# Attention values by whole rows, wider row projections, and half of each expert gather amid the gate/up products

## The chip, the cores and the metric

The kernel runs on one core of a Trainium2 chip. The metric is the device time of one execution in microseconds (us). The core has five engines that work side by side: TensorE (PE) for matrix products, VectorE (DVE), ScalarE (ACT), GpSimd (POOL) and SyncE (SP), whose queue issues nearly all transfers. Matrix products are written to PSUM and copied from there to SBUF by ACT or DVE.

## The reference

One layer of a hybrid decoder block over 512 tokens of width 1024, in float32:

```python
h = rmsnorm(x, g_mix);  proj = h @ w_in       # q, k, v, gates of both branches
o_g = gated_linear_attention(...)             # 4 heads, chunks of 64
o_m = moba_attention(...)                     # 8 heads of 64, blocks of 256, causal + top-3 past blocks
x = x + (sigmoid(z_g) * (o_g @ w_proj_gla) + sigmoid(z_m) * (o_m @ w_proj_moba)) @ w_out
x = x + memory_attention(rmsnorm(x, g_cross)) # 4 heads of 128 into 256 memory tokens
xt = rmsnorm(x, g_moe)                        # top-1 of 4 groups, top-2 of its 8 experts
for e in range(32):                           # for the tokens that chose expert e
    y[tok] += ((silu(xt[tok] @ w_gate[e]) * (xt[tok] @ w_up[e])) @ w_down[e]) * weight
out = rmsnorm(x + y, g_final)
```

The weights of the 32 experts (1024 x 512, 1024 x 512 and 512 x 1024 each) are 201 MB of the 252 MB that are moved.

## The kernel before

**Products.** Ordinary projections are made in three parts (`mm3`, lines 131 to 133): operands are split into a high part in the type fp32r and a rest, and high x high, rest x high and high x rest are added in PSUM. `in_feat` has weights as the stationary operand and 512 tokens moving (tiles `fo`). `in_rows` has 128 tokens as the stationary operand and the weights moving (tiles `ro0` to `ro3`); it goes over 256 columns at a time, in two loads of four k blocks (a k block is 128 of the 1024 features), and is called twice for the 512 columns of each of `vg`, `vm` and `vc`. `mm` (line 136) is a product in full float32; where its output has only 64 partitions (tiles `mo_ps`, `gu_ps`, `y_ps`), two such products lie side by side in the array's columns, which the rows show as `128*64`.

**Stages** on TensorE: rows and first projections to 39 us; projections woven with gated linear attention to 174; block attention (`moba`) woven with the gates' projections to 301; the two output projections, `w_out`, and memory attention with routing to 500; experts to the end.

**Block attention.** The items are 4 head pairs x 4 query tiles of 128. For each, `scores` (tile `s_ps`), a softmax on ACT and DVE, transposes of the probabilities (`ptp`), copies by ACT (`pt`), and `values` (`mo_ps`) for that query tile. The values of an item stand behind the scores of the next one. Between them the weaving puts products of the gates (`fo`).

**Experts.** The 32 experts are taken as 16 pairs p. Each expert has 64 slots, so a pair fills 128 partitions. `gate_up` makes gate and up products for one k block (`gu_ps`; 8 k blocks make 64 records). `hidden` (ACT, DVE) and `hidden_t` (four transposes `ht_ps` and a copy) follow, then `down` (`y_ps`, 32 records), a split into high and rest (`yh`, `yl`), and `combine`: for four token tiles and two column halves a product with the slots' rows (`c_ps`), added to x by DVE. The inputs of four experts are gathered at once by products with one-hot rows (`gather`: 8 chunks, one a k block, `g_ps`, copied to `xT`). For the experts of pairs p + 2 and p + 3, four chunks are made after the gate/up products of even pair p and four after those of pair p + 1, in alternation with the steps of `combine`, so that both cover `hidden`.

**Order of transfers.** A pair has 24 weight blocks of 512 KB, 384 in all, and each takes one of 48 buffers of the pool `blk`, which also holds other tiles. `eload(n)` lets SP issue all up to number n; it is called after k blocks and after `down` steps with `used + DEPTH + ...`, and for pair 0 with the list `D0`. The overflow loop (`overflow`, line 1268) handles experts with over 64 tokens; its count is read from memory into registers, and on the inputs here it runs zero times. It stands at the start of pair 15. The loads from number 368 on are held back until it is passed.

**Tail.** The last pair's `down` goes by two column halves. Each half has its own products and additions; squares are summed by ACT, the power of -1/2 is made on POOL (`rr`), and two stores of 256 KB go out for each token tile.

The routing codes are spread over all partitions by `c_bcast` (transposes `cb_ps` and copies), between the gate/up products of pair 0.

## Time and profile before

| what | value |
| --- | --- |
| median of 3 runs | 985.75 us (985.1 to 986.44) |
| the profiled execution | 985.1 us, with a span of 983.3 us on the core |
| TensorE busy | 961.1 us, 98% of the span, 5305 matmuls |
| VectorE, ScalarE, GpSimd busy | 474.8, 311.7, 32.7 us |
| moved by DMA | 252.52 MB, 257 GB/s over the span |

The span runs from the first to the last instruction. Busy time counts an engine as busy while at least one of its instructions is under way. Matmuls overlap, so the duration of a single one is longer than its distance to the next. PEld stands for the weight loads of TensorE, which lie beside its products.

### The profile page before, as it was taken

To read this page: it belongs to the slowest core of one execution; us is meant where nothing else is said; L and a number is where in the kernel's file an instruction comes from. 1 tells how busy PE (TensorE), PEld (TensorE's weight loads), DVE (VectorE), ACT (ScalarE), POOL (GpSimd) and SP (SyncE) were. 2 spreads that over 40 slices of the span, in tenths; PEclk is the share of its full clock that TensorE was granted. 3 is DMA by queue.
4 is the path that set the end of the run, shared out by engine and by line. 5 is a ranking of instruction groups with operands and counts; after the bars stand their busy time and mean duration, and the time that the engine had idled before them with its cause. 6 is when DMAs were issued, how large, how long until landed. Compare 5 with 4: busy or idle time off the path is not lost. (4 is left out here: it accounts for less than half of the span.)

```text
span 983.3 us, 13899 instructions
## 1 busy us (share of the span) xinstructions
PE 961.1 (98%) x5305; PEld 645.5 (66%) x5305; DVE 474.8 (48%) x1048; ACT 311.7 (32%) x631; POOL 32.7 (3%) x46
## 2 busy tenths in 40 slices
PE   9999999999999999999999999999999999999985
PEld 7889779888788888999844555544555554455432
DVE  6343863345555746566752543434453333444314
ACT  5452633445446424455521111111111111111003
POOL 3200010000000000000000000000000000000003
PEclk9999999999999999999999999999999999999998
DMA  9512347133133522644588999999999999999993
GB/s 300 160 44 58 71 65 193 44 86 86 60 133 129 176 81 67 198 190 196 200 331 329 409 408 409 409 409 408 409 409 409 409 408 409 409 409 409 409 383 148
DMA packets 117161, 252.52 MB, mean 257 GB/s; under 512 B 10310, under 2 KB 61795, under 8 KB 117092
## 3 DMA queue, kind: packets, MB, share of 16 engines
q1 hardware_dynamic: 117092, 251.60, 69.3%
q8 instruction: 43, 0.70, 0.3%
q14 instruction: 26, 0.21, 0.1%
HBM read 247.90 MB, written 3.67 MB: 256 GB/s over the span
## 5 line engine op out<-in xcount | busy, mean ns | idle before, releaser
L136 PE MATMUL gu_ps<-we,xT 128*64 128x512 f32 x1024 | 229.3, 597 | 5.1 <-PEq L1268 3.8
L136 PEld LDWEIGHTS gu_ps<-we,xT 128*64 128x64 f32 x1024 | 78.0, 138 | 150.5 <-issue 134.6
L213 DVE TENSOR_TENSOR wlo<-wraw,whi 128x1024 fp32r<-128x1024 f32 (+1 forms) x71 | 86.6, 1238 | 90.0 <-ACT whi L212 89.8
L136 PE MATMUL y_ps<-we,hid_t 128*64 128x512 f32 x512 | 114.2, 595 | 0.3 <-issue 0.3
L1229 DVE SCALAR_TENSOR_TENSOR hid<-hid,ws,gu_ps 128x512 f32<-128x512 f32 x16 | 11.9, 747 | 194.9 <-PE gu_ps L136 194.9
L1262 DVE TENSOR_TENSOR x<-c_ps,x 128x512 f32<-128x512 f32 x120 | 76.7, 685 | 38.9 <-PE c_ps L136 38.9
L131 PE MATMUL fo<-hTh,whi 128*128 128x512 f32 x224 | 90.5, 404 | 0.0
L133 PE MATMUL fo<-hTh,wlo 128*128 128x512 f32 x224 | 87.5, 391 | 0.0
L132 PE MATMUL fo<-hTl,whi 128*128 128x512 f32 x224 | 87.4, 390 | 0.0
L136 PEld LDWEIGHTS y_ps<-we,hid_t 128*64 128x64 f32 x512 | 36.3, 137 | 68.8 <-issue 55.7
L212 ACT ACTIVATE whi<-wraw 128x1024 fp32r<-128x1024 f32 (+2 forms) x73 | 74.5, 1043 | 1.9 <-DMA wraw<-in_w_in_dram 1.8
L1228 ACT ACTIVATE hid<-gu_ps 128x512 f32<-128x512 f32 x16 | 9.6, 597 | 197.5 <-PE gu_ps L136 197.5
L136 PE MATMUL g_ps<-oh,xrh 128*128 128x256 f32 x256 | 64.6, 293 | 1.7 <-DVE oh L1030 1.7
L136 PE MATMUL g_ps<-oh,xrl 128*128 128x256 f32 x256 | 61.6, 281 | 0.0
L136 PEld LDWEIGHTS g_ps<-oh,xrh 128*128 128x128 f32 x256 | 47.0, 189 | 14.9 <-PE gu_ps L136 9.7
L133 PE MATMUL ro<-whi,hTl 128*128 128x256 f32 (+1 forms) x192 | 55.4, 289 | 0.8 <-DVE hTl L333 0.8
L131 PE MATMUL ro<-whi,hTh 128*128 128x256 f32 (+1 forms) x192 | 56.0, 291 | 0.0
L132 PE MATMUL ro<-wlo,hTh 128*128 128x256 f32 (+1 forms) x192 | 55.5, 289 | 0.2 <-POOL wlo L213 0.2
L212 ACT ACTIVATE yh<-y_ps 128x512 fp32r<-128x512 f32 x32 | 19.1, 598 | 109.9 <-PE y_ps L136 109.9
L136 PE MATMUL c_ps<-yh,ot 128*128 128x512 f32 x128 | 50.8, 397 | 0.7 <-ACT yh L212 0.7
L136 PE MATMUL c_ps<-yl,ot 128*128 128x512 f32 x128 | 50.8, 397 | 0.2 <-DVE yl L213 0.2
L131 PEld LDWEIGHTS fo<-hTh,whi 128*128 128x128 f32 x224 | 42.0, 188 | 12.0 <-issue 3.9
(320 smaller groups left out, 1544.5 us busy)
## 6 DMA issues: line engine op xcount, KB each, us to landing
we<-in_w_exp_gate_dram SPq DMA_DIRECT2D x128, 512.0 KB, 10.2
we<-in_w_exp_up_dram SPq DMA_DIRECT2D x128, 512.0 KB, 10.2
we<-in_w_exp_down_dram SPq DMA_DIRECT2D x128, 512.0 KB, 10.2
wraw<-in_w_in_dram SPq DMA_DIRECT2D x38, 512.0 KB, 3.8
wraw<-in_w_out_dram SPq DMA_DIRECT2D x8, 512.0 KB, 6.1
wraw<-in_w_ckv_dram SPq DMA_DIRECT2D x8, 512.0 KB, 4.6
wraw<-in_w_proj_gla_dram SPq DMA_DIRECT2D x4, 512.0 KB, 3.9
wraw<-in_w_proj_moba_dram SPq DMA_DIRECT2D x4, 512.0 KB, 4.3
```

The source lines that it names most:

```text
L131: PE.matmul(o, lh, rh, start=first, stop=False)
L132: PE.matmul(o, lh, rl, start=False, stop=False)
L133: PE.matmul(o, ll, rh, start=False, stop=last)
L136: PE.matmul(o, l, r, start=first, stop=last, **kw)
L212: S.activation(hi, src, AF.Copy)
L213: eng.tensor_tensor(lo, src, f(hi), op=ALU.subtract)
L1228: S.activation(row, gu[0][0:n], AF.Silu)
L1229: V.scalar_tensor_tensor(row, row, ws[:, 0:1], gu[1][0:n], op0=ALU.mult, op1=ALU.mult)
L1262: V.tensor_tensor(xs, o, xs, op=ALU.add)
```

## The change

- `in_rows` goes over 512 columns at once, in four loads of two k blocks (`WIDE`).
- The mean square of the second token tile is made by ACT inside `to_feat`, not by DVE ahead of it.
- In block attention, the transposed probabilities of all query tiles of a head pair are kept (`pa`, `pb`), and `values` runs once per head pair, over all queries from key block j on.
- The broadcast of the codes begins between the two halves of the routing's last gather, and the tables of slots follow two k blocks earlier in pair 0.
- A gather belongs to an odd pair p and the pair after it: four chunks after the gate/up products of p, as before, and four ahead of the k blocks 0 to 3 in the gate/up products of p + 1. Pair 0 has no gather, and pair 14 has one's second half.
- `DEPTH` is 35 for pair 0 and 33 behind it. The overflow loop moves into pair 15, ahead of k = 2; its count is read at the start of pair 14, it has its own PSUM tiles, and loads from number 372 on are held back until it is passed.
- In the last pair the down weights are loaded by column halves; output goes by the column ranges 512, 256 and 256; the sums of squares have three parts; and one store of 512 KB goes out per token tile (two of 256 KB for the last).

The core of the diff (the removed lines of the old block attention and of the old tail are left out):

```diff
+    add_rows(w_in, 512, 512, WIDE)
...
-    def in_rows(n, evac, src, nt=NT, mark=None):
-        acc = [ps(f"ro{t}", [n]) for t in range(nt)]
-        for kh in range(2):
-            wh, wl = wnext(4, n)
+    def in_rows(evac, src, nt=NT, mark=None):
+        acc = [ps(f"ro{t}", [512]) for t in range(nt)]
+        kk = 0
+        for kn in WIDE:
+            wh, wl = wnext(kn, 512)
             for t in range(nt):
-                for k in range(4):
-                    kk = 4 * kh + k
-                    mm3(acc[t], src.hi[kk][:, tcol(t)], src.lo[kk][:, tcol(t)], wh[:, k, :], wl[:, k, :], kk == 0,
-                        kk == KD - 1)
-                    yield 0.33
-                if kh:
+                for k in range(kk, kk + kn):
+                    mm3(acc[t], src.hi[k][:, tcol(t)], src.lo[k][:, tcol(t)], wh[:, k - kk, :], wl[:, k - kk, :], k == 0,
+                        k == KD - 1)
+                    yield 0.65
+                if kk + kn == KD:
                     evac(t, acc[t])
+            kk += kn
...
+    def between():
+        r1.append(rms_scale(x_in[1]))
+        wsplit(2)
+    to_feat(xr, hT, 0, between)
+    rows[1] = scaled_rows(x_in[1], r1[0], gmix)
...
+        def transposed(i, res, pts):
+            for (pr, _), (pa, pb) in zip(res, pts):
                 t_ps = ps("ptp", [i + 1, P])
                 for j in range(i + 1):
                     PE.transpose(t_ps[:, j, :], pr[:, tcol(j)], ident)
+                n = min(i + 1, 2)
+                S.activation(pa[:, 0:n, tcol(i)], t_ps[:, 0:n, :], AF.Copy)
+                if i > 1:
+                    S.activation(pb[:, 0:i - 1, tcol(i - 2)], t_ps[:, 2:i + 1, :], AF.Copy)
+        def values(hp, pts):
+            o_ps = ps("mo_ps", [T])
+            for j in range(NT):
                 for half in range(2):
                     h = 2 * hp + half
                     sl = slice(64 * half, 64 * half + 64)
+                    pa, pb = pts[half]
+                    p_j = pa[:, j, j * P:] if j < 2 else pb[:, j - 2, (j - 2) * P:]
+                    mm(o_ps[sl, j * P:], vm[j][:, h * 64:(h + 1) * 64], p_j, j == 0, j == NT - 1, skip_group_check=True)
+            split(om.hi[hp], om.lo[hp], o_ps)
         items = [(hp, i) for hp in range(4) for i in range(NT)]
+        prev = None
         for hp, i in items:
             res = scores(hp, i)
+            if prev and i == 0:
+                values(*prev)
             yield 0.64 * FILL[i][0]
             normalise(i, res)
             yield 0.64 * FILL[i][1]
+            if i == 0:
+                prev = hp, [(blk("pa", [2, T]), med("pb", [2, 2 * P])) for half in range(2)]
+            transposed(i, res, prev[1])
         yield 1.0
+        values(*prev)
...
+    def load_down_halves(e):
+        for c in range(2):
+            for q in range(2):
+                b = blk("we", [2, 512])
+                rows = w_exp_down[0][e][2 * q * P:(2 * q + 2) * P, 512 * c:512 * c + 512]
+                SY.dma_start(b, rows.rearrange("(k p) n -> p k n", p=P))
+                yield b
...
-    eloads, elimit = [0], [12 * (NE - 2) + SPILL_AT]
+    eloads, elimit = [0], [SPILL[2]]
     def load_pairs():
         for p in range(NE // 2):
             pair = 2 * p, 2 * p + 1
-            for loads, n in ((load_gate_up, 2), (load_down, 1)):
+            for loads, n in ((load_gate_up, 2), (load_down_halves if p == NE // 2 - 1 else load_down, 1)):
...
+    bcast = c_bcast()
+    steps(bcast, 2)
     c_weights()
     c_gather(NT - 1)
...
+            if len(xT) == k:
+                xT.extend(rows2("xT", 4, ns))
+            o = to[k % 2] if to else ps("g_ps", [ns])
...
     NP = NE // 2
-    bcast, slot, spill = c_bcast(), None, spill_list()
+    slot, spill = None, spill_list()
     comb, gat = iter(()), iter(())
-    xT_next = None
     for p in range(NP):
         w = blocks[2 * p:2 * p + 2]
         used = 24 * p
-        if p == NP - 1:
-            eload(elimit[0])
-            overflow(*spilled)
-            elimit[0] = 12 * NE
-        eload(used + D0[0] if p == 0 else used + DEPTH)
-        if p % 2 == 0 and p:
-            xT = xT_next
+        depth = DEPTH[min(p, 1)]
+        if p == SPILL[0] - 1:
+            n_extra = nc.values_load(spilled[0][0:1, 0:1], min_val=0, max_val=NX - 1, skip_runtime_bounds_check_because=
+                                     "2 T assignments fill fewer than NX whole blocks")
+        eload(used + depth)
         gu = [ps("gu_ps", [512]) for q in range(2)]
         s0 = (p % 2) * P
         for k in range(KD):
+            if (p, k) == SPILL[0:2]:
+                overflow(n_extra, *spilled)
+                elimit[0] = 12 * NE
+            if p % 2 == 0:
+                steps(gat, 1)
             gate_up(gu, k, [xT[k][:, s0 + CAP * i:s0 + CAP * i + CAP] for i in range(2)], w)
             if k % 2:
-                eload(D0[1 + k // 2] if p == 0 else used + DEPTH + 2 * (k + 1))
+                eload(used + depth + 2 * (k + 1))
             if p == 0 and k >= BC_AT:
                 next(bcast, None)
-                if k == BC_AT + 3:
+                if k == BC_AT + 1:
                     slot = slot_rows(sid[:, 0:1])
-                    oh_next = group_hots(1)
-        if p % 2 == 0 and p + 2 < NP:
-            xT_next = rows2("xT", KD, 4 * CAP)
-            gat = gather(oh_next, xT_next, 4 * CAP)
+            if p % 2 and p + 1 < NP and k == OH_AT:
+                oh_next = group_hots((p + 1) // 2)
+        if p % 2 and p + 1 < NP:
+            xT = []
+            gat = gather(oh_next, xT, 4 * CAP)
         if p == NP - 1:
             gf = blk("gf", [D])
             SY.dma_start(gf, bcast_rows(g_final, D))
         hid = hidden(gu, slot[1])
-        gs = 4 if p + 2 < NP else 0
-        steps(gat, min(gs, 1))
+        gs = 1 if p % 2 and p + 1 < NP else 0
+        steps(gat, gs)
         steps(comb, 2 if gs else 4)
         hid_t = hidden_t(hid)
         for i in range(3):
-            steps(gat, min(gs, 1))
+            steps(gat, gs)
             steps(comb, 2)
         drain(comb)
         ot = slot[0]
         if p + 1 < NP:
             slot = slot_rows(sid[:, 2 * p + 2:2 * p + 3])
-        if p % 2 and p + 3 < NP:
-            oh_next = group_hots((p + 3) // 2)
         if p >= 2:
...
+    ranges = (0, 512), (512, 256), (768, 256)
...
     def scale(t):
+        V.tensor_tensor(s01[t], s01[t], ssq[t][:, 2:3], op=ALU.add)
+        G.tensor_tensor(r[t], s01[t], neghalf[:, 0:1], op=ALU.pow)
+    def low_half(t):
+        S.activation(xo[t][:, 0:512], xo[t][:, 0:512], AF.Copy, scale=r[t])
+    def high_half(t):
+        V.scalar_tensor_tensor(xo[t][:, 512:], x_sb[t][:, 512:], r[t], gf[:, 512:], op0=ALU.mult, op1=ALU.mult)
+    last_down(0, range(4))
+    high(0)
+    low(0)
+    last_down(1, range(4))
+    high(1)
+    low(1)
+    last_down(2, range(2))
+    o0 = products(0)
+    o1 = products(1)
+    last_down(2, range(2, 4))
+    for t in range(NT):
+        add(o0, 0, t)
+        if t == NT - 1:
+            high(2)
+        square(0, t)
+        gains(t)
+    for t in range(NT):
+        add(o1, 1, t)
+        square(1, t)
+        if t == 0:
+            low(2)
+    o2 = products(2)
+    for t in range(NT):
+        V.scalar_tensor_tensor(s01[t], ssq[t][:, 0:1], EPS, ssq[t][:, 1:2], op0=ALU.add, op1=ALU.add)
+        add(o2, 2, t)
+        square(2, t)
+        if t == 2:
+            scale(0)
+            low_half(0)
+    for t in range(NT):
+        high_half(t)
+        if t + 1 < NT:
+            SY.dma_start(out[tcol(t), :], xo[t])
+            scale(t + 1)
+            low_half(t + 1)
+    S.dma_start(out[tcol(t), 0:512], xo[t][:, 0:512])
+    SY.dma_start(out[tcol(t), 512:], xo[t][:, 512:])
...
+WIDE = 2, 2, 2, 2
+SPILL = 15, 2, 372
...
-DEPTH = 30
-D0 = 34, 37, 41, 44, 47
+DEPTH = 35, 33
+OH_AT = 3
```

TensorE's order in block attention, at the end of the first head pair; `ptp` are the transposes, `s_ps` the scores of the next item, `mo_ps` the values and `fo` the gates' products. Before, for query tile 3 (the last ahead of the next head pair):

```order
L133 MATMUL fo<-hTh_145,wlo 128x512
L679 MATMUL ptp<-keep,pr 128x128 x8
L136 MATMUL s_ps<-km_1092,qm_1412 128x256 x2
L136 MATMUL s_ps<-km_1093,qm_1412 128x256 x2
L136 MATMUL mo_ps<-pt,vm_1518 64x128 x4
L136 MATMUL mo_ps<-pt,vm_1519 64x128 x4
L131 MATMUL fo<-hTh_145,whi 128x512
L132 MATMUL fo<-hTl_149,whi 128x512
```

The change, for the same place, and behind it the place one query tile earlier:

```order
L133 MATMUL fo<-hTh_145,wlo 128x512
L675 MATMUL ptp<-keep,pr 128x128 x8
L136 MATMUL s_ps<-km_989,qm_1309 128x256 x2
L136 MATMUL s_ps<-km_990,qm_1309 128x256 x2
L136 MATMUL mo_ps<-pa,vm_1415 64x512 x2
L136 MATMUL mo_ps<-pa,vm_1415 64x384 x2
L136 MATMUL mo_ps<-pb,vm_1416 64x256 x2
L136 MATMUL mo_ps<-pb,vm_1416 64x128 x2
L131 MATMUL fo<-hTh_145,whi 128x512
```

```order
L133 MATMUL fo<-hTh_148,wlo 128x512
L675 MATMUL ptp<-keep,pr 128x128 x6
L136 MATMUL s_ps<-km_936,qm_1201 128x512 x2
L136 MATMUL s_ps<-km_937,qm_1201 128x512 x2
L131 MATMUL fo<-hTh_145,whi 128x512
L132 MATMUL fo<-hTl_149,whi 128x512
L133 MATMUL fo<-hTh_145,wlo 128x512
```

All values of the head pair now stand behind the first scores of the next one, eight products in a row over 512, 384, 256 and 128 columns in place of eight over 128, and behind the other query tiles' scores no values are left.

TensorE's order at the start of pair 2 (`y_ps` is the end of pair 1, `g_ps` a chunk of the gather). Before:

```order
L136 MATMUL y_ps<-we,hid_t 64x512 x16
L136 MATMUL gu_ps<-we,xT_5124 64x512 x16
L136 MATMUL gu_ps<-we,xT_5125 64x512 x16
L136 MATMUL g_ps<-oh,xrh_4067 128x256
L136 MATMUL g_ps<-oh,xrl_4071 128x256
L136 MATMUL g_ps<-oh,xrh_4068 128x256
L136 MATMUL g_ps<-oh,xrl_4072 128x256
L136 MATMUL g_ps<-oh,xrh_4069 128x256
```

The change:

```order
L136 MATMUL c_ps<-yh,ot 128x512
L136 MATMUL c_ps<-yl,ot 128x512
L136 MATMUL y_ps<-we,hid_t 64x512 x16
L136 MATMUL g_ps<-oh,xrh_3812 128x256
L136 MATMUL g_ps<-oh,xrl_3816 128x256
L136 MATMUL g_ps<-oh,xrh_3813 128x256
L136 MATMUL g_ps<-oh,xrl_3817 128x256
L136 MATMUL g_ps<-oh,xrh_3814 128x256
L136 MATMUL g_ps<-oh,xrl_3818 128x256
L136 MATMUL g_ps<-oh,xrh_3815 128x256
L136 MATMUL g_ps<-oh,xrl_3819 128x256
L136 MATMUL gu_ps<-we,xT_4950 64x512 x4
```

Eight gather products now stand ahead of each of the first four k blocks (`x4` are the four products of one k block), and none of them behind this pair's gate/up products.

SP's queue around the overflow loop, with the loads ahead of it. Before:

```order
L940 DMA we<-in_w_exp_up_dram 128x1024
L940 DMA we<-in_w_exp_gate_dram 128x1024
L940 DMA we<-in_w_exp_up_dram 128x1024
L1266 TENSOR_LOAD rt_xi
L1268 COMPARE_AND_BRANCH
L1268 UNCONDITIONAL_BRANCH
L1450 BRANCH_PREFETCH_HINT
L1269 ISA
L1269 TENSOR_LOAD rt_xi
```

The change:

```order
L935 DMA we<-in_w_exp_up_dram 128x1024
L935 DMA we<-in_w_exp_gate_dram 128x1024
L935 DMA we<-in_w_exp_up_dram 128x1024
L935 DMA we<-in_w_exp_gate_dram 128x1024
L1312 TENSOR_LOAD rt_xi
L935 DMA we<-in_w_exp_up_dram 128x1024
L935 DMA we<-in_w_exp_gate_dram 128x1024
L935 DMA we<-in_w_exp_up_dram 128x1024
L1273 COMPARE_AND_BRANCH
L1273 UNCONDITIONAL_BRANCH
L1496 BRANCH_PREFETCH_HINT
```

The read of the loop's count has moved ahead of the last three loads before the loop, and the loop's branch now stands behind four loads of pair 15.

## Rows read from the trace of the kernel before

**Rows 1.** The line of the page with the DMA rate in 40 equal slices of the span (24.6 us each), in GB/s.

```profile
GB/s 300 160 44 58 71 65 193 44 86 86 60 133 129 176 81 67 198 190 196 200 331 329 409 408 409 409 409 408 409 409 409 409 408 409 409 409 409 409 383 148
```

**Rows 2.** Busy time by stage: stretch in us, its length, then for PE, PEld, DVE, ACT and POOL the busy us with the number of instructions, the granted clock, the DMA share and GB/s. The stretches are block attention, the experts up to the last pair's y products, and the tail.

```profile
174.00:301.00 127.00, 125.99 (x711) 101.94 (x711) 62.30 (x211) 62.36 (x166) 0.00 (x0) 1.00 0.29 89
...
500.00:959.60 459.60, 453.90 (x2276) 216.96 (x2276) 181.99 (x373) 68.53 (x127) 0.00 (x0) 1.00 1.01 401
959.60:983.30 23.70, 12.32 (x49) 5.53 (x48) 10.85 (x21) 8.91 (x22) 7.59 (x8) 0.88 0.36 138
```

**Rows 3.** The same view for TensorE alone in two undisturbed stretches: the `vm` row projection (256 columns) and the `w_out` product (512 columns). Columns: length, busy us (records touched), granted clock, DMA share, GB/s.

```profile
153.94:176.97 23.03, 23.03 (x193) 1.00 0.49 128
345.08:366.85 21.77, 21.77 (x98) 1.00 0.28 77
```

**Rows 4.** Groups of instructions by line and shape in those two stretches: names, shape, count, busy us and mean ns of one, idle before.

```profile
L133 PE MATMUL ro<-whi,hTl 128*128 128x256 f32 x64 | 18.1, 283 | 0.0
...
L133 PE MATMUL xo<-whi,mTl 128*128 128x512 f32 x32 | 12.5, 389 | 0.0
```

**Rows 5.** Timeline of TensorE and ACT in block attention (start us, duration, engine, line, operation, and in brackets the idle time before with what ended it).

```profile
246.60 0.60 PE L136 MATMUL mo_ps<-pt,vm 128*64 128x128 f32 x4 [0.42 <-ACT pt L681]
...
270.65 1.09 ACT L681 ACTIVATE pt<-ptp 128x512 f32<-128x512 f32 x2 [0.94 <-PE ptp L679]
...
277.87 0.72 PE L136 MATMUL s_ps<-km,qm 128*128 128x256 f32 x4
278.52 0.46 PE L136 MATMUL mo_ps<-pt,vm 128*64 128x128 f32 x4
278.91 0.50 PE L131 MATMUL fo<-hTh,whi 128*128 128x512 f32 x1
279.25 0.39 PE L132 MATMUL fo<-hTl,whi 128*128 128x512 f32 x1
```

**Rows 6.** Timeline of DVE and TensorE at the start, where the first rows are projected.

```profile
10.80 0.74 DVE L333 TENSOR_TENSOR hTl<-tps,hTh 128x256 fp32r<-128x256 f32 x2
...
11.26 0.59 PE L133 MATMUL ro<-whi,hTl 128*128 128x272 f32 x1 [0.83 <-DVE hTl L333]
```

**Rows 7.** Timeline of TensorE around pair 0 of the experts.

```profile
499.89 5.37 PE L136 MATMUL gu_ps<-we,xT 128*64 128x512 f32 x24
505.20 0.65 PE L1073 MATMUL cb_ps<-keep,rt_code 128*128 128x128 f32 x4
505.78 1.94 PE L136 MATMUL gu_ps<-we,xT 128*64 128x512 f32 x8
507.64 0.65 PE L1073 MATMUL cb_ps<-keep,rt_code 128*128 128x128 f32 x4
...
516.71 0.39 PE L136 MATMUL g_ps<-oh,xrh 128*128 128x256 f32 x1
...
522.38 7.09 PE L136 MATMUL y_ps<-we,hid_t 128*64 128x512 f32 x32
529.29 13.90 PE L136 MATMUL gu_ps<-we,xT 128*64 128x512 f32 x64
```

**Rows 8.** Timeline of TensorE, DVE and ACT from the end of pair 1's gate/up products to pair 2's.

```profile
543.13 0.39 PE L136 MATMUL g_ps<-oh,xrh 128*128 128x256 f32 x1
...
543.30 0.75 DVE L1229 SCALAR_TENSOR_TENSOR hid<-hid,ws,gu_ps 128x512 f32<-128x512 f32 x1 [12.44 <-PE gu_ps L136]
...
545.11 0.60 PE L1235 MATMUL ht_ps<-keep,hid 128*128 128x128 f32 x4
545.47 0.36 PE L136 MATMUL g_ps<-oh,xrh 128*128 128x256 f32 x1
...
545.75 0.60 ACT L1237 ACTIVATE hid_t<-ht_ps 128x512 f32<-128x512 f32 x1 [0.89 <-PE ht_ps L1235]
...
551.28 7.09 PE L136 MATMUL y_ps<-we,hid_t 128*64 128x512 f32 x32
558.20 13.90 PE L136 MATMUL gu_ps<-we,xT 128*64 128x512 f32 x64
```

**Rows 9.** Busy time of TensorE in the gate/up products of pairs 12 to 15, and in two us of pair 15 (columns as in rows 3).

```profile
847.56:862.13 14.57, 14.57 (x66) 1.00 1.03 409
877.17:892.83 15.66, 15.11 (x66) 1.00 1.03 409
907.90:923.67 15.77, 15.12 (x66) 1.00 1.03 410
938.86:955.29 16.43, 16.43 (x64) 0.90 1.00 388
940.00:942.00 2.00, 2.00 (x6) 0.50 0.92 340
```

**Rows 10.** Timeline of TensorE, POOL and DVE in the last pair and the tail.

```profile
938.86 16.50 PE L136 MATMUL gu_ps<-we,xT 128*64 128x512 f32 x64 [3.77 <-PEq L1268]
...
959.63 5.98 PE L136 MATMUL y_ps<-we,hid_t 128*64 128x512 f32 x24
...
974.10 1.07 POOL L1382 TENSOR_TENSOR rr<-ms,neghalf 128x1 f32<-128x1 f32 x2 [1.95 <-DVE ms L1380]
...
974.69 0.75 DVE L1387 SCALAR_TENSOR_TENSOR xo<-x,rr,gf 128x512 f32<-128x512 f32 x1 [0.59 <-POOL rr L1382]
```

More of the change, by code (lines that the diff above doesn't have):

```diff
@@ L204, in block_kernel @@
     add_feat(w_cq, 0, 4)
-    for j in range(2):
-        add_rows(w_ckv, 512 + 256 * j, 256)
+    add_rows(w_ckv, 512, 512, WIDE)
     for c in range(2):
@@ L1085, in block_kernel @@
     c_exp(1)
-    steps(vgen, 16)
+    steps(vgen, 8)
     c_normalise(0)
@@ L1263, in combine, with overflow @@
                 yield t, c
-    def overflow(xi, xb):
-        n_extra = nc.values_load(xi[0:1, 0:1], min_val=0, max_val=NX - 1,
-                                 skip_runtime_bounds_check_because="2 T assignments fill fewer than NX whole blocks")
+    def overflow(n_extra, xi, xb):
         with tc.For_i(0, n_extra, 1, iteration_sync='staggered') as i:
@@ L1289, in overflow @@
                     gate_up(gu, k, xT[k:k + 1], [{2 * j + q: w[q] for q in range(2)}])
-            hid_t = hidden_t(hidden(gu, ws, CAP, hid), CAP)
-            y_ps, load = [ps("y_ps", [512]) for c in range(2)], load_down(bass.ds(e, 1), to)
+            hid_t = hidden_t(hidden(gu, ws, CAP, hid), CAP, pb[4][:, 0:4 * CAP].rearrange("p (a n) -> p a n", a=4))
+            y_ps, load = pb[0:2], load_down(bass.ds(e, 1), to)
             for ft in range(4):
@@ new lines, in block_kernel, with x_part, y_part, last_down @@
+    ssq, xo = [small("ss3", [3]) for t in range(NT)], [blk("xo", [D]) for t in range(NT)]
+    s01, r = [small("ss4", [1]) for t in range(NT)], [small("rr", [1]) for t in range(NT)]
+    def x_part(i, t):
+        a, n = ranges[i]
+        return x_sb[t][:, a:a + n]
+    def y_part(i):
+        a, n = ranges[i]
+        return y_ps[a // 512][:, a % 512:a % 512 + n]
+    def last_down(i, fts):
+        a, n = ranges[i]
+        c, a = divmod(a, 512)
+        for ft in fts:
+            for e, (b, own) in enumerate(zip(w, halves)):
+                mm(y_ps[c][own, a:a + n], hid_t[:, ft, 64 * e:64 * e + 64], b[8 + 2 * c + ft // 2][:, ft % 2, a:a + n],
+                   ft == 0, ft == 3, skip_group_check=True)
@@ new lines, in block_kernel, with high, low, products @@
+    y = [[med(q, [n], F32R) for q in ("yh", "yl")] for _, n in ranges]
+    def high(i):
+        S.activation(y[i][0], y_part(i), AF.Copy)
+    def low(i):
+        V.tensor_tensor(y[i][1], y_part(i), f(y[i][0]), op=ALU.subtract)
+    def products(i):
+        n = ranges[i][1]
+        o = [ps("c_ps", [512 // n, n]) for _ in range(NT * n // 512)]
+        o = [b[:, q, :] for b in o for q in range(512 // n)]
+        for t in range(NT):
+            product(o[t], ot, t, y[i])
+        return o
```

119 lines of the change are left out of this document (22 added, 97 removed).

## The prediction

> **What bounds the kernel now.** I first read the busy time of each engine by stage [rows 2]. TensorE is busy for 125.99 of 127.00 us in the block-attention stage and for 453.90 of 459.60 us in the expert stage, and it waits only at a few places. So a term counts if it changes how fast TensorE's stream runs, or one of its stops. Next comes the line of GB/s [rows 1]: from the 23rd slice on the weights arrive at 408 to 409 GB/s with hardly a gap. TensorE and the weights run neck and neck in the expert stage, and each gain there must be held against the other. Third, the late pairs [rows 9]: the 64 gate/up records of one pair take 13.84 us where nothing is late (529.29 in [rows 7] to 543.13 in [rows 8]), but 14.57, 15.66, 15.77 and 16.43 us in pairs 12 to 15. That is 7.1 us over the undisturbed time, and the weights are late there. Ahead of pair 15 stands a stop of 3.77 us at the overflow loop [rows 10], and in 940 to 942 us the granted clock is 0.50, that is 1.2 of 2.4 GHz [rows 9]. The profiled span is 983.3 us and this execution took 985.1, so 1.8 us lie outside. The median of the runs is 985.75, 0.65 above it. I add the sum to the median.
>
> **How to read TensorE's rows.** Durations overlap, so a price is the distance from one start to the next. 192 matmuls of 256 columns fill 23.03 us, 0.120 each, and 96 of 512 columns fill 21.77 us, 0.227 each [rows 3], though single ones are listed at 283 and 389 ns [rows 4].
>
> **1. Row projections 512 wide: -3.15 us.** 192 + 192 + 96 matmuls of 256 columns become 240 of 512: 480 x 0.120 = 57.6 against 240 x 0.227 = 54.4. Loads keep their number and size, and splits their work. Bounds 0 (if a split comes late) and -3.2. The listed durations would give 480 x 0.283 - 240 x 0.389 = 42.5 us. That reading is wrong, since the same rows would then need 54 us for a window of 23.03.
>
> The Trainium skill (TensorE: Matmul & The Clock Gate, section Single matmul latency) puts one matmul at (398 + N) / 2.4 ns. That is 272 and 379 ns, near the listed durations, and by it the term would be 39.6 us. The section Back-to-back issue gap of that page puts the distance at N / 2.4 + 2.5 ns, 109 and 216, by which it would be 0.6 us. The measured distances of 120 and 227 ns lie above both, and the sum goes by them.
>
> **2. Attention values once per head pair: -5.2 us.** The columns stay the same, but 12 of 16 visits to the 64-column form go away. One visit costs, beyond its columns [rows 5]: the four value records take 0.39 us (278.52 to 278.91) for 4 x 128 columns, which at 0.216 per 512 are 0.22, so 0.17 extra. The first fo after it takes 0.34 instead of 0.23, so 0.11. The scores ahead take 0.65 for 4 x 256 columns, 0.48, so 0.17, which may belong to the change of data type that stays. That makes 0.28 to 0.45 a visit. I take 0.37, and 12 x 0.37 = 4.4. A value record now and then waits for its copy (0.42 at 246.60). The copies of the first three query tiles lose their hurry, for which I estimate 1.2, three such places at 0.4 each. Against it the last tile needs four copies instead of two (1.09 us for two); behind 0.65 us of scores I let 0.1 a head pair show, 0.4. Bounds -2.5 and -6.6.
>
> **3. Mean square of the second tile on ACT: -0.5.** TensorE waits 0.83 us at 11.26 for hTl, which DVE begins at 10.80 behind that mean square [rows 6]. Bounds 0 and -0.9.
>
> **4. Broadcast of the codes: +1.45 ahead of the experts.** Eight transposes at 0.09 (four take 0.36, 545.11 to 545.47 [rows 8]) make 0.72, plus one copy that xT waits behind, an estimate with bounds 0.7 and 2.
>
> **5. Pair 0: -4.8.** It takes 29.40 now (499.89 to 529.29 [rows 7]). One interruption by four cb transposes costs 505.20 to 507.64, 2.44, less eight gate/up records of 0.216, which is 0.71 us. Two of the four leave, so gate/up takes 13.84 + 1.42 = 15.26. Without a gather nothing covers the hidden row. From [rows 8], DVE ends 0.92 after the last gate/up record (543.30 + 0.75 against 543.13), ht follows at 1.05, its copy ends 1.24 after that, and with 0.1 to spare y starts at 2.4. y takes 6.92 (551.28 to 558.20). Sum 24.6. The four chunks of this gather are not gone; the last gather's second half now lies in pair 14: 32 x 0.12 plus a switch, **+4.0**.
>
> **6. Half of each gather amid gate/up: +9.8.** In an even pair from 2 to 14 TensorE goes from 64-column products to full-width ones and back five times instead of once. A round trip is the interruption of term 5 without its own work: 0.71 - 0.36 = 0.35. 7 x 4 x 0.35 = 9.8. Bounds: 0.20 each (only the first g after gate/up, 0.10, and the way back), 5.6, and 0.45 as in term 2, 12.6. The copies of the chunks out of PSUM (some 0.6 us each, as that of hid_t in [rows 8]) have 1.7 us of gate/up beside them and are hidden; uncovered they would cost up to 28 x 0.6 = 17 us.
>
> The Trainium skill (TensorEngine Tiling (Array Packing), section Key Properties) says that a change of the tiling mode drains the array. It speaks against this edit and gives no price; the trace has one in the 0.35 above.
>
> **7. Deeper loads: -7.1.** The 7.1 us over in pairs 12 to 15 [rows 9] go if the weights come 4 to 6 us earlier against TensorE. They lost some 4.8 us in each of the slices at 331 and 329 GB/s (24.6 x 80 / 409), around pair 0, where loads waited for blocks that pair 0 and its gather held. Pair 0 is now shorter, holds fewer blocks and asks for one to three more. The slower even pairs add margin. Bounds -3 and -7.1.
>
> **8. Overflow loop in pair 15 behind two k: -1.9, then +0.9.** The registers are read a pair earlier. I halve the stop of 3.77 us [rows 10], with bounds of 1.3 and 3.8 for what is left, both estimates. SP is now stopped after load 371 instead of 367, until TensorE is two k into pair 15, so the queue runs dry for some 5 us; I charge 0.9 for a late weight at k = 6.
>
> **9. The tail: +0.3.** From the first y of the last pair (959.63 [rows 10]) to the end there are 23.7 us. Won: 0.7 of a wait for the last weight, and about 1 from a last range of 256 instead of 512 columns. Lost: the power on POOL (1.07 for two) now stands between one tile's last square and its 0.75 us on DVE, tile by tile, about 1.5 us a tile instead of 1.0. Bounds -1.5 and +2.
>
> **Sum.** -3.15 - 5.2 - 0.5 + 1.45 - 4.8 + 4.0 + 9.8 - 7.1 - 1.9 + 0.9 + 0.3 = -6.2, so 985.75 - 6.2 = **979.5 us**. The expert stage is nearly even (+1.2), and the gain is made ahead of it.
>
> **Rivals.**
> (a) *The switches are cheap.* At 0.20 each, term 6 is 5.6, and the time 975.3. For it: one part of the round trip is a gap of only 0.10. Against it: [rows 7] show the whole. Below that the weights bind: about 973.
> (b) *The loop costs what it did.* A stop of 3.9 again (+1.9) and half clock behind it again (16.43 x (1 - 0.90) = 1.6, which is part of the 7.1 in term 7): 983.0. For it: [rows 9, 10]. Against it: the registers are loaded early.
> (c) *The weights bind the end.* If term 7 brings only 3 and the dry queue costs 2 more: 979.5 + 4.1 + 2 = 985.6, no change.
> (d) *Slower: the values wait.* All four copies of a head pair's last tile stand on ACT ahead of all its values, behind the gates' work. If TensorE stands s us there each time, the gain is gone at s = 1.55, and at 2.5 the time is 989.5. For it: TensorE already waits 0.42 for one such copy [rows 5]. Against it: ACT is busy for only 62.36 of 127 us [rows 2].
>
> **Numbers.** The measurement tells 0.2% (2 us) from no change. The sum 0.50 (own range 977 to 982.5), (a) 0.20, (b) 0.15, (c) 0.07, (d) 0.08. Faster: 0.50 + 0.20 + two thirds of (b) = 0.80. Same: the rest of (b) and most of (c), 0.11. Slower: 0.09. The range 972 to 986 takes in all but (d) and the far end of (a).
>
> **What the profile after will show.** 1: v rows of 96 matmuls in 21.8 us. 2: the block-attention stage some 5 us shorter, with four value segments of about 2.4 us. 5: pair 0 in 24.6. 6: even pairs 1.4 us longer than odd ones. 7: gate/up of pairs 12 to 14 free of waits. 8: a stop under 3 us inside pair 15. I am wrong if even pairs are as long as odd ones, if the late pairs still wait, or if the gain ahead of the experts is under 6 us.

## The result, and the profile after

The changed kernel takes 979.11 us (median of 4 runs, 978.45 to 980.16), against 985.55 for the kernel before, measured beside it (4 runs, 985.1 to 986.44). The ratio is 0.9935, with a 95% interval of [0.9917, 0.9952]: 0.65% faster. The forecast was 979.5, faster. The profiled execution took 979.03 us with a span of 977.2, so the span is 6.1 us shorter. Each experiment below has its own measurements of the kernel before beside it, to which its ratio is taken; their medians lie between 984.79 and 985.36 us. A difference of under 1 us between two variants is therefore read from the traces and not from the times.

From the page of the changed kernel: the span, the busy time of the engines, and the DMA rate in 40 slices (24.4 us each).

```profile
span 977.2 us, 13312 instructions
PE 955.9 (98%) x4993; PEld 623.6 (64%) x4993; DVE 473.0 (48%) x1056; ACT 313.5 (32%) x648; POOL 32.2 (3%) x46
...
GB/s 295 168 44 65 65 61 185 57 83 91 61 182 127 193 21 132 135 276 133 256 315 409 409 409 409 409 409 409 409 409 409 409 409 409 409 409 409 409 307 129
...
L136 PE MATMUL gu_ps<-we,xT 128*64 128x512 f32 x1024 | 229.2, 595 | 0.7 <-ACT xT L1051 0.3
```

TensorE is still busy for 98% of the span. The full rate of 409 GB/s begins one slice earlier than in [rows 1], and the 39th slice falls to 307 (it was 383), because the last loads are held back until the loop. By the listed idle times the gate/up products stood for 0.7 us in the whole run. Before, pair 15's alone stood 3.77 [rows 10].

The stretches of the changed kernel on TensorE. Columns as in [rows 3]. In order: the `vm` projection, block attention from its first scores to the first output projection, memory attention's output up to the first gate/up product, pair 0, an odd pair, the even pair behind it, two stretches of pair 15, and the tail from the last pair's first y.

```profile
152.62:174.38 21.76, 21.76 (x98) 1.00 0.60 157
174.38:294.16 119.78, 118.80 (x593) 1.00 0.31 96
441.31:493.30 51.99, 49.73 (x344) 1.00 0.49 182
493.30:517.91 24.61, 22.99 (x109) 1.00 0.96 370
577.19:606.18 28.99, 28.99 (x150) 1.00 1.03 409
606.18:636.35 30.17, 30.17 (x150) 1.00 1.03 409
930.00:935.00 5.00, 5.00 (x26) 1.00 0.51 206
935.00:940.00 5.00, 5.00 (x26) 1.00 0.68 231
952.00:977.20 25.20, 11.94 (x73) 0.83 0.35 137
```

Three stretches of the kernel before that no row above has: block attention between the same two points, 25 us around the end of its pair 0, and the stretch up to its first gate/up product.

```profile
176.97:301.43 124.46, 123.45 (x691) 1.00 0.30 92
520.00:545.00 25.00, 25.00 (x129) 1.00 0.88 340
448.98:499.89 50.91, 48.85 (x336) 1.00 0.50 187
```

TensorE's longest stop in block attention of the changed kernel, ahead of the transposes of the probabilities:

```profile
201.95 0.63 PE L675 MATMUL ptp<-keep,pr 128*128 128x128 f32 x4 [0.33 <-DVE sm L666]
```

TensorE of the changed kernel in the last pair and the tail. Start us, duration, operation, idle before.

```profile
932.15 11.32 PE L136 MATMUL gu_ps<-we,xT 128*64 128x512 f32 x50
943.67 1.08 PE L136 MATMUL gu_ps<-we,xT 128*64 128x512 f32 x4 [0.20 <-DMA we<-in_w_exp_gate_dram]
944.95 2.79 PE L136 MATMUL gu_ps<-we,xT 128*64 128x512 f32 x10 [0.20 <-DMA we<-in_w_exp_up_dram]
...
952.00 5.38 PE L136 MATMUL y_ps<-we,hid_t 128*64 128x512 f32 x32
958.33 1.08 PE L136 MATMUL y_ps<-we,hid_t 128*64 128x256 f32 x8 [0.94 <-DVE yl L1388]
```

The 50 records from 932.15 to 943.47 run across the loop's place without a gap that the trace names, and the clock is 1.00 throughout. The stop of [rows 10] is gone. In its place there are two waits of 0.20 for weights, and a new stop of 0.94 in the tail. From start to start the two waits cost more than they are listed with. All gate/up products of pair 15, and two us around the loop's place:

```profile
932.15:947.67 15.52, 15.12 (x67) 1.00 0.76 269
934.00:936.00 2.00, 2.00 (x12) 1.00 0.10 35
```

They take 15.52 us where 13.84 would do, and the 1.7 us lie at k = 6, the first k block whose loads were held back: the queue had run almost empty (35 GB/s).

Where the span went, term by term, as distances between the same two instructions in both traces (us):

| term | forecast | measured | from |
| --- | --- | --- | --- |
| 1 wide rows | -3.15 | -3.05 | `vg` -1.17, `vm` 23.03 to 21.76, `vc` -0.61 |
| 2 values | -5.2 | -4.7 | 124.46 to 119.78 |
| 3 start | -0.5 | -0.2 | first rows done at 39.69 instead of 39.88 |
| 4 broadcast | +1.45 | +1.1 | 50.91 to 51.99 |
| 5 pair 0; chunks in pair 14 | -4.8; +4.0 | -4.8; +3.8 | 29.40 to 24.61; 32 x 0.12 |
| 6 amid gate/up | +9.8 | +9.7 | 7 x (59.16 - 57.78), two pairs after and before |
| 7, 8 late weights, loop | -8.1 | -9.2 | 4.5 of waits in pairs 12 to 14, 3.77, 16.43 to 15.52 |
| 9 tail | +0.3 | +1.5 | 23.67 to 25.20 |

The sum of the right column is -5.9, and the span lost 6.1. The rows are no closed account: ahead of pair 0 they add up to 6.85 where the first gate/up product comes 6.59 us earlier (499.89 to 493.30), and from there to the last pair's first y they add up to 0.5 where 1.0 was won (459.74 to 458.70). The 3.8 for the chunks in pair 14 is worked out and not measured.

### The profile page after: what moved, and what is told of

It is laid out like the page before. It is cut to its first block, busy times and chain, and to the rows that moved or that the text cites. A ratio compares the mean times of both kernels' runs of the same rounds, so it can differ in the third digit from the quotient of the medians.

```text
span 977.2 us, 13312 instructions
## 1 busy us (share of the span) xinstructions
PE 955.9 (98%) x4993; PEld 623.6 (64%) x4993; DVE 473.0 (48%) x1056; ACT 313.5 (32%) x648; POOL 32.2 (3%) x46
## 4 chain that ended last, share of the span: by engine, by line
PE 91%; DVE 3%; ACT 2%; DMA 2%; issue 1%; SPq 1%; POOL 0%; POOLq 0%; DVEq 0%; ACTq 0%
PE gu_ps L136 22%; PE y_ps L136 12%; PE fo L131 7%; PE fo L133 7%; PE fo L132 7%; PE g_ps L136 7%; PE c_ps L136 6%; PE ro L133 2%; PE ro L131 2%; PE ro L132 2%; PE x2o L136 2%; PE xo L132 1%; PE xo L133 1%; PE xo L131 1%; PE o_ps L136 1%; PE mo_ps L136 1%
## 5 line engine op out<-in xcount | busy, mean ns | idle before, releaser
L136 PEld LDWEIGHTS gu_ps<-we,xT 128*64 128x64 f32 x1024 | 70.9, 137 | 134.7 <-issue 121.5
L136 PE MATMUL y_ps<-we,hid_t 128*64 128x512 f32 (+1 forms) x528 | 113.9, 583 | 1.6 <-DVE yl L1388 0.9
L1209 ACT ACTIVATE xT<-g_ps,gfeat 128x256 f32<-128x256 f32 x56 | 25.8, 474 | 89.2 <-PE g_ps L136 57.6
L136 PE MATMUL c_ps<-yh,ot 128*128 128x512 f32 (+1 forms) x132 | 52.4, 399 | 0.5 <-ACT yh L1385 0.5
L136 PE MATMUL c_ps<-yl,ot 128*128 128x512 f32 (+1 forms) x132 | 51.0, 388 | 0.1
L133 PEld LDWEIGHTS fo<-hTh,wlo 128*128 128x128 f32 x224 | 42.1, 188 | 9.1
L136 PEld LDWEIGHTS g_ps<-oh,xrl 128*128 128x128 f32 x256 | 47.1, 189 | 0.6
```

What stands on the lines that cost most here:

```text
L133: PE.matmul(o, ll, rh, start=False, stop=last)
L136: PE.matmul(o, l, r, start=first, stop=last, **kw)
L1209: S.activation(xT[k], o, AF.Copy, scale=gfeat[:, k:k + 1])
```

## Experiments: what a visit amid gate/up costs

The theory: each return from the gather to the gate/up products costs 0.35 us, so the same eight chunks in fewer visits save that much per visit left out. The rival: the cost belongs to the chunks or their copies, and stays.

**Two visits of two chunks** instead of four of one.

```diff
-            if p % 2 == 0:
-                steps(gat, 1)
+            if p % 2 == 0 and k in (0, 2):
+                steps(gat, 2)
```

> Four chunks amid the gate/up products as in the changed kernel, but two ahead of k = 0 and two ahead of k = 2. By the price of a visit (0.345 us) even pairs are 0.69 shorter and the time is 4.8 us shorter, 974.3. If the price lies in the chunks (their copies, their weight loads) and not in the visit, nothing changes: 979.

Measured: 975.43 us, 0.9904 [0.9888, 0.9921]. An odd and an even pair of this run on TensorE:

```profile
576.87:605.89 29.02, 29.02 (x151) 1.00 1.03 409
605.89:635.38 29.49, 29.49 (x151) 1.00 1.03 410
```

The two take 58.51 us, 0.65 less for two visits fewer: 0.33 each. Over seven even pairs that is 4.6 us, of which 3.6 arrived in the span; 0.5 went to gate/up of pair 15, which took 16.03 instead of 15.52, with one wait of 0.51 for weights, and 0.35 was lost ahead of the experts (pair 0 begins at 493.65).

**Seven visits**: the four chunks amid gate/up in seven pieces.

```diff
                     mm(o, src[t][:, tcol(k)], oh[:, t, :], t == 0 and q == 0, t == NT - 1 and q == 1)
+                if k >= 4 and t == 1 and not to:
+                    yield
...
-            if p % 2 == 0:
-                steps(gat, 1)
+            if p % 2 == 0 and k < 7:
+                steps(gat, 2 if k == 6 else 1)
```

> The four chunks are cut into halves, which stand ahead of k = 0 to 6 (two halves ahead of k = 6): seven visits in place of four. By the price of a visit even pairs are 1.03 longer and the time is 7.2 us longer, 986.3. If weights or copies set the pace of these pairs, less than 2 us longer.

Measured: 986.57 us, 1.0013 [1.0004, 1.0023]. The same two pairs:

```profile
578.48:607.47 28.99, 28.99 (x151) 1.00 1.03 409
607.47:638.66 31.19, 31.19 (x151) 1.00 1.03 409
```

Only the even pair grew, by 1.02 for three visits, 0.34 each; seven times 1.02 on 979.11 is 986.3, and the time agrees. With the same chunks, products and copies the time rises and falls with the number of visits. The rival is out. What is priced is the round trip as a whole: the gather's products differ from the gate/up products in form (`128*128` and `128*64` in the rows) and in operand type (fp32r and full float32), and no run here parts the two.

**One visit** of all four chunks.

```diff
-            if p % 2 == 0:
-                steps(gat, 1)
+            if p % 2 == 0 and k == 0:
+                steps(gat, 4)
```

> All four chunks of the second half ahead of k = 0 of the even pair: one visit in place of four, 21 fewer. By the price of a visit (0.33 us) the time is 7.0 shorter, 972.1, less what the weights take back: two visits gave 3.7 of 4.6, so I expect 973 to 974. If a wait for copies or blocks arises, as with the whole gather in the cover, it is longer than the changed kernel.

Measured: 975.32 us, 0.9897 [0.9880, 0.9913], no faster than with two visits. Two pairs took 58.16, so the visits gave 7.0 us, but only 3.8 arrived. TensorE in pair 15, and 5 us of it:

```profile
925.47 7.89 PE L136 MATMUL gu_ps<-we,xT 128*64 128x512 f32 x34
934.34 1.08 PE L136 MATMUL gu_ps<-we,xT 128*64 128x512 f32 x4 [0.98 <-DMA we<-in_w_exp_gate_dram]
935.62 2.79 PE L136 MATMUL gu_ps<-we,xT 128*64 128x512 f32 x12 [0.20 <-DMA we<-in_w_exp_up_dram]
939.45 1.08 PE L136 MATMUL gu_ps<-we,xT 128*64 128x512 f32 x4 [1.03 <-DMA we<-in_w_exp_gate_dram]
...
930.00:935.00 5.00, 4.02 (x19) 1.00 1.03 400
```

TensorE reaches pair 15 6.7 us earlier than in the changed kernel, the queue is full (400 GB/s, where the changed kernel shows 206 in 930 to 935), and gate/up takes 18.00. The weights bind the end here. That is the edge of rival (a), which put it at about 973 us.

## Experiments: all eight chunks behind the odd pair

The theory: TensorE has time enough under the odd pair's `hidden` and `combine` for all eight chunks, so the visits can be left out altogether at no price but the chunks' own.

**All chunks in the cover.**

```diff
-        steps(gat, gs)
+        steps(gat, 2 * gs)
...
-            steps(gat, gs)
+            steps(gat, 2 * gs)
```

> All eight chunks of a gather stand behind the gate/up products of the odd pair, two where one stood, and none amid gate/up. If a visit to full-width products costs 0.345 us (two pairs took 59.16 us in the changed kernel and 57.78 before, so 1.38 for four visits), 28 visits less give -9.7, and the weights, now nearer, take some 2 back: 970 to 972 us, odd pairs near 32.8 and even ones near 25. If the weights bind the stage, the late pairs' gate/up products wait again, by 5 us or more in all, and the time is 975 or more.

Measured: 990.48 us, 1.0064 [1.0045, 1.0082]. The expectation missed by 18 us, on the other side of the kernel before. ACT in the odd pair:

```profile
597.28 0.48 ACT L1209 ACTIVATE xT<-g_ps,gfeat 128x256 f32<-128x256 f32 x1 [0.48 <-PE g_ps L136]
605.06 1.57 ACT L1209 ACTIVATE xT<-g_ps,gfeat 128x256 f32<-128x256 f32 x4 [7.29 <-PE g_ps L136]
```

After four copies the fifth waits 7.29 us, until all eight chunks are made: it lacks a place to write to. An odd and the even pair behind it take 59.9 us (577.96 to 637.87) against 59.16: the odd pair takes 34.84 instead of 32.8, as TensorE stops twice for 0.78 us there, and that is more than the visits gave. In three of the seven odd pairs the granted clock falls to 0.50 behind these stops, and the pair takes 36.36. TensorE in an odd pair of either kind:

```profile
577.96:612.80 34.84, 33.27 (x183) 1.00 1.03 409
757.71:794.07 36.36, 34.79 (x182) 0.95 1.03 410
```

7 x 0.75 for the pairs and 3 x 1.52 for the clock make 9.8 of the 10.5 us by which the span is longer than the changed kernel's.

**Space for all eight inputs taken ahead.**

```diff
-            xT = []
+            xT = rows2("xT", KD, 4 * CAP)
```

> As the run with all eight chunks in the odd pair's cover, but both blocks for the gathered inputs are taken ahead of the first chunk. There the fifth chunk's copy waited 7.3 us, until TensorE had ended the eighth chunk, and PSUM ran full behind it. If the late-taken block is the cause, the wait is gone, odd pairs take near 32.8 and even ones near 25, and the time is 970 to 973. If ACT or PSUM can't carry two chunks a step, the wait stays and the time is near 990. Where the weights bind, the late pairs' gate/up products wait again, 4 us or more in all.

Measured (with the cover edit above): 993.35 us, 1.0077 [1.0056, 1.0098]. Missed again, and the wait stayed as it was:

```profile
604.98 1.21 ACT L1209 ACTIVATE xT<-g_ps,gfeat 128x256 f32<-128x256 f32 x3 [7.30 <-PE g_ps L136]
```

As I read the program's memory map, the second half of the inputs now lies where the gather's own one-hot rows lie, so it can't be written before the last chunk is made. TensorE has the same two stops in each odd pair, and the clock falls in four of the seven.

**Two buffers more for them**, with shallower loads.

```diff
-DEPTH = 35, 33
+DEPTH = 35, 31
```

> As the run with all eight chunks in the odd pair's cover and both input blocks taken first, with one number changed: loads are asked for 31 blocks ahead, not 33. With 33 the pool is full, and the second block for the inputs is laid where the gather's own one-hot rows lie, which its last chunk still reads; with 31 it has a place of its own. If that caused the stop, odd pairs fall from 36 to about 33 us, the time falls from 993 to the neighbourhood of the run with one visit, 973 to 976, and then the weights bind: gate/up of the last pairs waits 5 us or more in all. If two chunks a step are too many for ACT or PSUM, it stays near 990.

Measured (on top of the two edits above): 993.31 us, 1.0068 [1.0049, 1.0088]. Missed a third time. ACT's copies, TensorE's stops, two us of the clock, and the whole odd pair:

```profile
599.17 0.47 ACT L1209 ACTIVATE xT<-g_ps,gfeat 128x256 f32<-128x256 f32 x1 [1.40 <-PE g_ps L136]
...
604.42 0.47 ACT L1209 ACTIVATE xT<-g_ps,gfeat 128x256 f32<-128x256 f32 x1 [3.81 <-PE g_ps L136]
...
601.34 0.50 PE L136 MATMUL c_ps<-yh,ot 128*128 128x512 f32 x1 [0.78 <-DVE x L1269]
602.86 0.39 PE L136 MATMUL g_ps<-oh,xrh 128*128 128x256 f32 x1 [0.78 <-DVE x L1269]
...
604.00:606.00 2.00, 2.00 (x11) 0.50 1.02 406
...
577.97:614.33 36.36, 34.79 (x183) 0.95 1.03 408
```

The fifth copy now comes on time (599.17), so the missing place in SBUF was real. But it had cost TensorE nothing: here too TensorE stops twice for 0.78 us until DVE has added a `combine` product to x, and an odd pair takes 34.85 us, or 36.36 where the clock falls to 0.50 behind the stops, as in the two runs above. With the four chunks moved in, 29.0 + 3.8 = 32.8 would do. The profiled spans of the three runs (987.7, 989.0 and 991.9) differ as the number of pairs in which the clock falls: three, four and six, 1.5 us each. As I read the program's map of PSUM, six chunks and the hidden rows hold seven of eight tiles, so that products of `combine` and the next chunk share the last one and each waits for the copy out of it. The waits fit that reading; I did not run a variant with freed PSUM tiles, so this last cause is read, not shown.

## Experiments: the late weights and the loop

**Depth as before.**

```diff
-DEPTH = 35, 33
+DEPTH = 30, 30
```

> Loads are asked for as far ahead as before (30 blocks) in place of 35 and 33; all else as in the changed kernel. If the depth brought the late pairs' gate/up products back to 13.8 us (term 7), they wait again by 3 us or more, and the time is 982 or more. If the margin comes from a shorter pair 0 and longer even pairs, no wait returns and the time is 979 to 980.

Measured: 979.47 us, 0.9943 [0.9926, 0.9961], not told apart from the changed kernel. Pairs 12 to 14 have no waits, and gate/up of pair 15 takes 15.88. TensorE and the DMA around pair 0 in this run:

```profile
490.00:515.00 25.00, 23.04 (x120) 1.00 0.81 305
515.00:540.00 25.00, 25.00 (x134) 1.00 1.03 409
```

After its pair 0 the queue runs at 409, where the kernel before had 340 in 520 to 545: (409 - 340) x 25 / 409 = 4.2 us of loading won, with loads no deeper than before. SP's issues say the same: the first weights of pair 15 are asked for at 922.26 us before, at 910.23 in the changed kernel and at 911.25 here, while pair 0 begins 6.6 us earlier than before in both. So the queue gained 5.4 and 4.4 us on TensorE, and the depth is worth 1.0 of it; the deeper loads are not the cause of the gain. What remains, by elimination, is the shorter pair 0 without a gather, and the 1.4 us that each even pair became slower. The run with one visit takes the second away, and there waits are back (pair 13's gate/up takes 14.24). No run puts the gather back into pair 0, so its share is argued and not shown.

**The count read late**, right ahead of the loop.

```diff
-        if p == SPILL[0] - 1:
-            n_extra = nc.values_load(...)
...
             if (p, k) == SPILL[0:2]:
+                n_extra = nc.values_load(...)
                 overflow(n_extra, *spilled)
```

> The changed kernel with the loop's count read right at the loop, not a pair earlier. If the read was the stop of 3.8 us in the kernel before, TensorE stops some 3 us or more in pair 15, the weights behind it come as much later, and the time is 982 to 984. If it was the place of the loop (between two pairs), there is no stop and the time is 979.

Measured: 979.88 us, 0.9939 [0.9923, 0.9956]; the profiled span is 979.2, 2.0 longer, but that was the longest of the four executions (979.14 to 981.01), and by its time the run is not told apart from the changed kernel. TensorE in pair 15:

```profile
932.03 3.60 PE L136 MATMUL gu_ps<-we,xT 128*64 128x512 f32 x16
935.82 7.91 PE L136 MATMUL gu_ps<-we,xT 128*64 128x512 f32 x34 [0.18 <-PEq L1273]
945.63 1.08 PE L136 MATMUL gu_ps<-we,xT 128*64 128x512 f32 x4 [1.91 <-DMA we<-in_w_exp_gate_dram]
```

Even with the read right ahead of it, TensorE stops for only 0.18 at the loop, not 3.77. In this execution the next weights come 1.7 us later instead (1.91 against 0.20), and SP issues the first four held loads from 935.83 to 937.89 where it was 935.33 to 936.91. So the early read is worth up to 2 us by way of the queue, and the stop of before belonged to the loop's old place, or to what the queue was doing there.

## Experiment: the tail

The products that add the first range (`products(0)`) are issued ahead of all products of the third range, not behind half of them.

```diff
-    last_down(2, range(2))
     o0 = products(0)
+    last_down(2, range(2))
     o1 = products(1)
```

> The changed kernel with one line moved in the tail: the products of the first 512 columns ahead of the first half of the third range's down products. If TensorE's stop of 0.94 us there (it waits for the second range's low part, which DVE reads out of the same PSUM tile) costs its length, the time is 1.0 us shorter, 978.1. If the tail hangs on the tile-by-tile chain of sums, powers and scalings, it is 979 as before.

Measured: 978.08 us, 0.9922 [0.9905, 0.9938]. TensorE in its tail:

```profile
952.62 5.38 PE L136 MATMUL y_ps<-we,hid_t 128*64 128x512 f32 x32
957.93 0.50 PE L136 MATMUL c_ps<-yh,ot 128*128 128x512 f32 x1
...
959.98 1.08 PE L136 MATMUL y_ps<-we,hid_t 128*64 128x256 f32 x8
```

The sums now run where the stop of 0.94 was, and from the first y to the end it takes 976.5 - 952.62 = 23.9 us instead of 25.2. The time fell by 1.0, as gate/up of pair 15 took 16.20 instead of 15.52 in this execution. In the changed kernel the third range's products wait for the low part of the second range, which is still being read from the same PSUM tile.

## Experiments: two parts undone

**Row projections of 256 columns**, in loads of four k blocks, as before the change.

```diff
-        acc = [ps(f"ro{t}", [512]) for t in range(nt)]
+        acc = [ps(f"ro{t}", [n]) for t in range(nt)]
...
-    add_rows(w_in, 2576, 512, WIDE)
+    for j in range(2):
+        add_rows(w_in, 2576 + 256 * j, 256)
...
```

The same is done for `vg` and `vc`.

> The changed kernel with the row projections back at 256 columns in two passes. By the distances of 0.120 and 0.227 us the time is 3.1 us longer, 982.2, all of it in the three row projections; by the listed durations it would be 42 us longer. If the weights bind the end, a later start of the experts costs less than 3.

Measured: 981.64 us, 0.9962 [0.9948, 0.9976]. `vm` is back at its old length, as in [rows 3]:

```profile
153.64:176.68 23.04, 23.04 (x194) 1.00 0.52 139
```

The time rose by 2.5. The experts begin 2.75 us later (496.05), and pair 15's gate/up is 0.9 shorter, since the weights had more time.

**Values per query tile**, as before the change.

```diff
-            if prev and i == 0:
-                values(*prev)
+            if prev:
+                finish(*prev)
...
```

`finish` makes the values of one query tile out of a tile `pt` of its own, as in the kernel before.

> The changed kernel with the attention values back at one query tile each. The block-attention stage measured 124.46 us before (first scores to the first output projection) and 119.78 with the change: the time is 4.7 us longer, 983.8. Each of the twelve visits more should cost 0.28 to 0.45 us. If part of the gain came from elsewhere (a shorter wait for weights), less than 3.

Measured: 984.13 us, 0.9988 [0.9978, 0.9997], 5.0 slower than the changed kernel. Block attention is back at before's 124.46:

```profile
174.81:299.26 124.45, 123.44 (x690) 1.00 0.31 93
```

## Experiment: the good parts together

Two visits and the tail's order, with the edits shown above, and the loop two k blocks later.

```diff
-SPILL = 15, 2, 372
+SPILL = 15, 4, 376
```

> Two visits in place of four, the line moved in the tail, and the overflow loop two k later (ahead of k = 4, loads from number 376 on held back until it). The first gave 3.7 us (975.4) and the second 1.0; where the queue ran short for 0.8 us at the held loads, the third may give up to 0.8 back. If they add up: 973.6 to 974.4. If the weights bind the whole end, the tail's 1.0 stays and the rest is nothing: 974.4; if the stop at the loop returns there, 976 or more.

Measured: 976.88 us, 0.9919 [0.9905, 0.9932]. It missed, and is not better than two visits alone. TensorE in pair 15 and its clock behind the loop:

```profile
927.61 8.33 PE L136 MATMUL gu_ps<-we,xT 128*64 128x512 f32 x36
938.67 6.64 PE L136 MATMUL gu_ps<-we,xT 128*64 128x512 f32 x22 [2.74 <-issue]
...
940.00:942.00 2.00, 2.00 (x6) 0.50 0.99 371
```

A stop of 2.74 us stands behind the loop again, "issue" names nothing that releases it, and half clock follows, as in [rows 9, 10]. The queue was busy around both long stops (371 GB/s behind this one, 340 in [rows 9]) and half empty where there was none (206 to 231 in the changed kernel). But the run with one visit had a full queue and its longest stop was 1.03, put down to weights, so the cause of this stop stays open. One candidate, untested here, is that TensorE's instructions behind the loop's branch come late; the views don't show how they come. The stop may not come each time: of the five executions the one of 975.36 us has a mean clock of 0.996, the four of 976.59 to 977.83 one of 0.993 or 0.994. The best kernels of this study are those with one and with two visits, 975.3 and 975.4 us, 1.0% below the kernel before.

## Why the prediction was right, and where it was not

**The sum held because TensorE's stream was the bound**, and terms 1, 2, 5 and 6 are parts of that stream, priced by distances between starts.
1. *Wide rows*: -3.15 forecast, -3.05 measured; undone alone it costs 2.5 in time. The distances of 0.120 and 0.227 were the right reading. The listed durations would have been wrong by 39 us.
2. *Values*: within 0.5. Undone, block attention took the 4.7 longer again and the time 5.0. The rival that the values wait for their copies (d) did not come. Idle time is 0.98 us in 174.38 to 294.16 and was 1.01, but it is not the same idle time. Before, the values stood for ACT's copies (0.42 in [rows 5], 0.30 at 299.92). These waits are gone, as the term had it, and in their place the transposes, now reached earlier, stand for the softmax on DVE, which the term left out; the longest stop is the 0.33 at 201.95. So what arrived came from the visits: 4.7 / 12 = 0.39 each against 0.37.
3. *Start*: 0.2 of the 0.5 came. The wait of 0.83 for hTl is gone, but one of 1.08 us for `wlo`, behind POOL, stands at 10.71 in its place, and at 19.45 TensorE waits for hTl again (0.21). Before, products of 272 columns followed each other every 0.23 us up to 14.83 and every 0.13 behind it; the prediction read the stop and not this pace.
4. *Broadcast*: 1.1, inside its bounds.
5. *Pair 0*: 24.61 for a forecast of 24.6.
6. *Visits*: 0.345 each against 0.35, confirmed at one, two, four and seven visits. The price came from one interruption by transposes in pair 0 and held for an interruption by another product of full width. The Trainium skill (TensorEngine Tiling (Array Packing), section Key Properties) says that a change of tiling mode drains the array. These runs agree in that each round trip costs time, 0.33 to 0.35 us here; they don't show the draining itself. Rival (a) with 0.20 is out.

**Three steps failed, and their misses cancelled.** The loop gave 1.9 us more than forecast, the late weights took 0.8 more and the tail 1.2 more. That the total came within 0.4 us is luck in this part.
7. *Deeper loads*: the size (-7.1) was near, since the waits of pairs 12 to 14 are gone, but the cause that heads the term is wrong. Depth 30 gives the same time. What the term names second is what is left: the shorter pair 0, with which the queue reaches 409 a slice earlier, and the slower even pairs, which give the weights time.
8. *Loop*: I left half of the stop, 1.9, and gave the early read as the reason. The changed kernel has none, and the late read has 0.18. So rival (b) is out in this kernel, and the early read works, if at all, through SP's queue. The 0.9 for the dry queue was too low: the listed waits are only 0.4, but from start to start gate/up of pair 15 takes 1.7 us more than 13.84, all of it at k = 6.
9. *Tail*: +0.3 forecast, +1.5 measured. I counted the chain of 1.5 us a tile, and that is there: POOL's `rr` begin at 967.25, 968.79, 970.34 and 971.83. What I missed is the 0.94 that the third range waits for the second's PSUM tile; moving one line takes 1.3 us of the tail away again.

Rival (c) did not come: in the changed kernel TensorE waits for no weights but those held back at the loop. But some 4 us more of speed bring them back, as the run with one visit shows.

## What to carry to other kernels

Price a switch between product shapes by the interruption that the trace already has, start to start, less its own work; then count visits, since grouping the same work into fewer visits costs nothing as long as nothing waits for it. Before filling a cover with more work, count the tiles that this work holds at once, in SBUF and in PSUM: three runs that moved 3.8 us of work a time under a cover ended 11 to 14 us above the changed kernel. The missing place in SBUF cost TensorE nothing; two short stops in each pair did, which fit a full PSUM (read, not shown), and the slower clock that sometimes followed them. And where two resources run neck and neck, expect each gain beyond the margin (here about 4 us) to come back as a wait of the other.

## What the runs showed of the hardware that I had not expected

- The granted clock fell to 0.50 (1.2 of 2.4 GHz) behind a stop of 3.77 us ([rows 9, 10]) and one of 2.74 us, and stayed at 1.00 behind single stops of 0.94, 1.03 and 1.91 us (in the tail of the changed kernel, with one visit and with the late read). In the cover runs it fell in some of the seven odd pairs and not in others with the same order of work: in six with the depth of 31, in four with the space ahead, in three of the first run. Two rows of the first cover run, behind the two stops of 0.78 us in an early odd pair and behind the same place in a later one:

```profile
604.00:606.00 2.00, 2.00 (x15) 1.00 1.02 408
...
784.00:786.00 2.00, 2.00 (x10) 0.50 1.01 404
```

- A loop that runs zero times cost TensorE 3.77, no visible gap, 0.18, or a stop of 2.74 behind it, in four kernels that differ in its place, in when its count is read and in how busy the queue is; I could not tie it to one cause.
